# GLA level products for two chunks at once: every second chunk kept backwards and interleaved with its neighbour

## The chip, the core and the metric

The kernel runs on one core of a Trainium2 chip. The metric is the device time of one execution in microseconds (us). The engines are named as in the profile: PE is TensorE (matrix products), PEld its weight load, DVE VectorE, ACT ScalarE, POOL GpSimd, SP the engine that issues all DMAs here.

## What is computed

One inference step of a hybrid decoder layer for 1024 prompt tokens and 8 single sample tokens, all in fp32. Two branches run in parallel, gated linear attention (GLA, 4 heads, key width 128, value width 256) and RWKV-7 (16 heads of 64), and are merged by gates, projected out and normalised.

```python
p = einsum('btd,dn->btn', x, w_in)                      # 1024 -> 9360 columns
p_gla, p_rwkv, p_gate = split(p)
q, k, v, g_a, a_lr = split(p_gla)                       # 512, 512, 1024, 1024, 16
log_a = log_sigmoid(a_lr @ gla_alpha_w2 + gla_alpha_b) / 16
# GLA:    S_t = diag(a_t) S_{t-1} + k_t^T v_t ;  o_t = q_t S_t
# chunked: A[i,j] = sum_d q[i,d] k[j,d] exp(b[i,d] - b[j,d]) for j <= i, b = cumsum(log_a)
#          o = A v + (q exp(b)) S
o_gla = rmsnorm(o_gla) * gla_norm_w * silu(g_a)
# RWKV-7: S_t = S_{t-1}(diag(w_t) - kk_t^T (kk_t a_t)) + v_t^T k_t ;  y_t = S_t r_t
o_rwkv = (groupnorm(y) + bonus) * silu(g_b)
m = sigmoid(gate_a) * (o_gla @ w_up_gla) + sigmoid(gate_b) * (o_rwkv @ w_up_rwkv)
y = layernorm(ALPHA * x + m @ w_out)
```

The final GLA and RWKV states and the last projected RWKV row are outputs too.

## The kernel before

**Halves and stages.** Tokens lie along the free dimension, channels on the partitions. The tokens are done in two halves (`PASS`, line 29): half 0 has 512 prompt tokens and the 8 samples, cut into two tiles of 260 columns; half 1 has 512 prompt tokens in one tile. For each half the plan (`make_plan`, line 1558) lists blocks of 128 output channels of the input projection: RWKV rows, GLA rows (q, k, two of v for each head, later two of the gate g), and the merge gates, which are stored in DRAM (`gate_row`). Each block is 24 fp32r products per token tile (operands are split in a high and a low part: 8 slices of 128 x 3). After both halves of the input projection come the up-projections (GLA half 0, RWKV half 0, GLA half 1, RWKV half 1), then the output projection.

**The order of the work.** It is decided by a planner written in the kernel (`Order`, line 238): each activity is a stream (a Python generator) that yields operations; at each step the planner takes the operation with the best start by its own prices and priorities, and issues it. So any change of an operation moves the order on all engines. All operations are issued from one helper, which is why nearly every line of the profile says L216: groups are told apart by the tiles that they write and read. All DMAs go through SP's queue, in order. Each engine executes its own instructions in order. Buffers are counted: 31 rows of 128 x 520 ("row"), PSUM banks "proj" (2), "big" (3), "pch" (1), "pY" (2).

**One GLA head** (`gla_head`, line 752) runs when its q, k, v rows are projected, one head at a time. It computes the decay a (tile `al`), then the lower triangle AT of the attention matrix of each of four chunks of 128 tokens (`GC`), in levels m = 1, 2, 4, ..., 64 (`LEVELS`). At level m the chunk is cut into blocks of 2m tokens; the queries of a block's second half meet the keys of its first half, each scaled by the decays up to the middle. Afterwards q and k are scaled on to the next level in place. The level's product takes all 128 keys of a chunk as the stationary operand and the 64 queries of the second halves as the moving one:

```python
for x in range(NGC if lv else 0):
    qc = qp_[:, x * P:(x + 1) * P].rearrange("p (b two m) -> p b two m", two=2, m=m)
    yield self.P.matmul(pl[:, x], km_[:, x * P:(x + 1) * P], qc[:, :, 1, :], start=True, stop=True)
```

Half of the stationary operand (the keys of second halves) is of no use in it. The result's useful blocks are written into AT with a mask (`copy_predicated`, mask `lev`) for m = 1 to 8 (`MASKED = 4`), and block by block for 16, 32 and 64: 4 + 2 + 1 copies. The diagonal and level 1 come without a product, from sums of q x k on VectorE. After the levels, for each chunk: transposes of v and k (`vk`), the products AT x v, S x q and k x v, and the state S.

**The up-projection** (`up_row`, line 1420) multiplies each block's result by a gate. `load_gates` (line 1404) fetches the gates from DRAM once the front parts of all eight RWKV pairs (`fronts`) and all gate rows (`gated`) of half 1 are done, and while 8 rows are spare; a block is not issued before its gate's load is (`yield lambda: self.gts`).

Of the kernel before, what the change touches and what calls it, by code (L numbers as in the profile page):

```python
# [12 lines left out]
I32 = mybir.dt.int32  # L13
U8 = mybir.dt.uint8
AF = mybir.ActivationFunctionType
ALU = mybir.AluOpType
AP = bass.AP
# [10 lines left out]

PASS = [(0, HT + NS, NS, [(0, 260), (260, 260)]), (HT + NS, HT, 0, [(0, 512)])]
GH, GDK, GDV = 4, 128, 256  # L30
# [29 lines left out]
RAWS = 4  # L60
SPARE_ROWS = 8


# [23 lines left out]
LEVELS = [1, 2, 4, 8, 16, 32, 64]  # L87
MASKED = 4
GLA_EPS = 1e-5
# [20 lines left out]
def constants():  # L110
    c = np.zeros((P, CST_W), np.float32)

    def put(name, v):
        o, w = CST[name]
        c[:, o:o + w] = v

    i = np.arange(P)
    put("ident", np.eye(P))
    s, t = i[:, None] % C, i[None, :] % C
    put("gmask", np.concatenate([s < t, s <= t], axis=1))  # L120
    lev = np.zeros((P, 64 * MASKED), np.uint8)
    for n, m in enumerate(LEVELS[:MASKED]):
        ri = np.array([x for x in range(P) if (x // m) % 2 == 1])
        j = i[:, None]
        lev[:, 64 * n:64 * n + 64] = ((j // (2 * m)) == (ri[None, :] // (2 * m))) & ((j // m) % 2 == 0)
    return c, lev, ((i[:, None] // C) == (i[None] // C)).astype(np.float32)
# [277 lines left out]
class Kern(Order):  # L404
# [71 lines left out]
    def setup(self):  # L476
# [42 lines left out]

        self.lev = cp.tile([P, 64 * MASKED], U8, name="lev")  # L520

# [221 lines left out]

    def gla_row(self, c, rows, scale):
        x = yield from self.row(c.n, KEEP)
        rows.append(x)

        def ev(tt, t0, w, q):
            yield self.A.activation(x[:, t0:t0 + w], q, AF.Copy, scale=scale)
        return ev  # L750

    def gla_head(self, c, h, rows, g):
# [11 lines left out]
        for t0, w in c.tiles:  # L764
            pz = yield from self.bank("big", [P, w])
            yield self.P.matmul(pz, self.gw2[:, h * GDK:(h + 1) * GDK], self.alr[:, t0:t0 + w], start=True, stop=True)
            yield A.activation(z[:, t0:t0 + w], pz, AF.Identity, bias=self.pvec("gab", h))
            self.free(pz)
# [5 lines left out]

        AT = AT_.rearrange("p (c t) -> p c t", c=NGC)
        yield E.memset(AT, 0.0)
# [4 lines left out]
        yield E.tensor_mul(u, q[:, :HT], k[:, :HT])  # L781
# [3 lines left out]
        yield E.tensor_mul(u[:, 0::2], km_[:, 0::2], qp_[:, 1::2])  # L785
        yield V.transpose(w, u)
# [4 lines left out]
        for i in range(4):  # L791
            yield V.tensor_add(dd[b[i], :, 0:NGC], r2[b[0], :, i::4], r2[b[2], :, i::4])
        dd = dd[:, :, 0:NGC].unsqueeze(3)
        yield V.copy_predicated(AT, self.ident.bitcast(I32).unsqueeze(1).to_broadcast([P, NGC, P]),
                                dd[:, 0].to_broadcast([P, NGC, P]))
        tot = al[:, :HT]
        for lv, m in enumerate(LEVELS):
            nb = P // (2 * m)
            pl = (yield from self.bank("big", [P, NGC, nb, m])) if lv else None
            wide = lv < MASKED  # L800
# [3 lines left out]
            mk = self.lev[:, 64 * lv:64 * lv + 64] if wide else None  # L804
            av = AT.rearrange("p c (b two m) -> p c b two m", two=2, m=m)
            if m == 1:
                out, dat, mk = av[:, :, :, 1, 0], dd[:, 1].to_broadcast([P, NGC, 64]), \
                    mk.unsqueeze(1).to_broadcast([P, NGC, 64])
            elif wide:
                out, dat = av[:, :, :, 1, :], pl  # L810
                mk = mk.rearrange("p (b m) -> p b m", m=m).unsqueeze(1).to_broadcast([P, NGC, nb, m])
            nt = HT // (2 * m)
            tv = tot.rearrange("p (b two) -> p b two", two=2)
            qv = qp_.rearrange("p (b two m) -> p b two m", two=2, m=m)
            kv = km_.rearrange("p (b two m) -> p b two m", two=2, m=m)
            nt_ = al[:, :nt]
            yield E.tensor_mul(kv[:, :, 0, :], kv[:, :, 0, :], tv[:, :, 1:2].to_broadcast([P, nt, m]))
            yield E.tensor_mul(qv[:, :, 1, :], qv[:, :, 1, :], tv[:, :, 0:1].to_broadcast([P, nt, m]))
            yield E.tensor_mul(nt_, tv[:, :, 0], tv[:, :, 1])
            if wide:  # L820
                yield V.copy_predicated(out, mk, dat)
            else:
                for b in range(nb):
                    s = slice(2 * m * b, 2 * m * b + m)
                    yield self.C.copy(av[s, :, b, 1], pl[s, :, b])
            self.free(*([pl] if lv else [r, r2, dd]))
            tot = nt_


        def vk(x):  # L830
            s = slice(x * P, (x + 1) * P)
            pt = yield from self.bank("big", [P, 3 * P])
            yield self.tr(pt[:, 0:P], v[0][:, s])
            yield self.tr(pt[:, P:2 * P], v[1][:, s])
            yield self.tr(pt[:, 2 * P:], km_[:, s])
            VK = vks[x % 2][:, :3 * P]
            yield A.copy(VK, pt)
            self.free(pt)
            return VK
        VK = yield from vk(0)  # L840
        for x in range(NGC):
            s = slice(x * P, (x + 1) * P)
            VKn = (yield from vk(x + 1)) if x < NGC - 1 else None
            pb = yield from self.bank("big", [P, 4, P])
            po, pS = pb[:, 0:2], pb[:, 2:4].rearrange("p a b -> p (a b)")
            for j in range(2):
                yield self.P.matmul(po[:, j], VK[:, j * P:(j + 1) * P], AT[:, x], start=True, stop=(S is None))
                if S is not None:
                    yield self.P.matmul(po[:, j], S[:, j * P:(j + 1) * P], qp_[:, s], start=False, stop=True)
# [708 lines left out]
    def make_plan(self):  # L1558
        w_in = self.a["w_in"]
        for c in self.ctx:  # L1560
# [15 lines left out]
            for p in range(NPAIR):  # L1576
# [9 lines left out]
                if p % 2 == 0:  # L1586
# [3 lines left out]
                    for n, (off, scale) in enumerate(offs):  # L1590
                        self.add(c, lambda c=c, rows=rows, scale=scale: self.gla_row(c, rows, scale), w_in, off,
                                 (lambda c=c, h=h, rows=rows, g=c.gg[h]:
                                   self.spawn(self.gla_head(c, h, rows, g), "head")) if n == 3 else None)
# [24 lines left out]
    def run_all(self):  # L1618
        self.chained, self.headed, self.decayed = -1, 0, 0
        self.first = ["wa", "x0", "w0", "x1", "x2", "x3", "w1", "x4", "x5", "x6", "x7", "pv", "shift", "w2", "w3", "cst"]  # L1620
        self.has = set()
        self.sampled = self.w_done = False
        self.plan, self.xq, self.ws, self.wo, self.gts, self.l2s = [], [], [], [], [], []
        self.setup()
# [70 lines left out]
```

## Time and profile before

| | us |
|---|---|
| median of 3 runs | 1623.23 |
| lowest, highest | 1619.05, 1623.53 |
| span of the profiled execution | 1622.0 |

No other time is given for the profiled execution than its span; the median lies 1.2 us above it. The mean granted TensorE clock is 0.995.

How to read the profile: a group's row has line, engine, operation, written<-read tiles and shapes, the count, then busy time and mean ns of one, then the idle time before it and what ended it. A row of waits has the engine and tile, what it waited for, then total us, times and the longest. A timeline row has start, duration, engine, operation and, in brackets, the idle time before it. A row of windows has busy time and instruction count of each engine in a stretch. Recorded durations of products overlap, since they are pipelined; what a product costs is read from the distance between starts. One fp32 product appears as two passes, one fp32r product as one.

### The profile page before, as it was taken

Reading aid. Unit: us, or ns where it says so; the run is one execution under the profiler, and the core shown is the slowest. Engines: PE = TensorE matmul, PEld = TensorE weight load, DVE = VectorE, ACT = ScalarE, POOL = GpSimd, SP = SyncE. Lnnn points to the kernel's source line nnn. Section 1 sums busy time; section 2 is a strip of 40 time slices with the busy share of each in tenths; the row PEclk is TensorE's granted clock in tenths of the full one; section 3 lists DMA queues with packets and bytes.
Section 4 is the critical chain, followed back from the end, with each engine's and each line's share of the span. In section 5 each row is a group of like instructions: output and inputs, shape, how many; then the busy total and the mean of one; then the engine's idle time right before and its main releaser. Section 6 shows DMA issues by size and latency. Waiting matters only on the chain.

```text
span 1622.0 us, 29342 instructions
## 1 busy us (share of the span) xinstructions
PE 1571.4 (97%) x10066; PEld 1393.9 (86%) x10066; DVE 1273.1 (78%) x3349; ACT 821.4 (51%) x1929; POOL 124.3 (8%) x205
## 2 busy tenths in 40 slices
PE   8999999999999999999999999999999989999998
PEld 6999999899999998778888877778788879988786
DVE  6788888788888988878777898788886785765555
ACT  5555655566566656553644464436444545544210
POOL 1001200101000001000000011111000100000000
PEclk9999999999999999999999999999999999999999
DMA  9766765587577657664465436644654577888432
GB/s 303 241 216 216 249 224 183 194 275 244 179 227 254 231 170 255 210 177 113 143 200 165 140 123 193 188 135 133 208 170 118 159 223 235 262 286 270 140 112 84
DMA packets 206641, 318.27 MB, mean 196 GB/s; under 512 B 87204, under 2 KB 102573, under 8 KB 206493
## 3 DMA queue, kind: packets, MB, share of 16 engines
q1 hardware_dynamic: 206492, 316.40, 61.3%
q8 instruction: 80, 1.31, 0.3%
q14 instruction: 69, 0.56, 0.1%
HBM read 196.66 MB, written 118.61 MB: 194 GB/s over the span
## 4 chain that ended last, share of the span: by engine, by line
PE 45%; DVE 9%; DMA 6%; ACT 2%; SPq 2%; issue 2%; POOL 0%; POOLq 0%; DVEq 0%; ACTq 0%
PE proj L216 21%; PE big L216 15%; PE pY L216 6%; PE pch L216 3%; DVE Xt L216 2%; DVE row L216 2%; DMA wide<-LD 2%; DVE X L216 2%; SPq L216 2%; DVE wide L216 1%; ACT row L216 1%; DMA wpart<-w 0%; DMA row<-xT 0%; DMA o_gla<-row 0%; DMA wraw<-w_up_gla 0%
## 5 line engine op out<-in xcount | busy, mean ns | idle before, releaser
L216 PE MATMUL proj<-xh,wpart 128*128 128x260 f32 (+1 forms) x3760 | 919.8, 328 | 2.3 <-DMA wpart<-w 2.1
L216 PEld LDWEIGHTS proj<-xh,wpart 128*128 128x128 f32 x3760 | 626.6, 189 | 52.3 <-issue 5.6
L216 PE MATMUL proj<-xl,wpart 128*128 128x260 f32 (+1 forms) x1880 | 618.1, 329 | 0.4 <-DVE xl L216 0.3
L216 PEld LDWEIGHTS proj<-xl,wpart 128*128 128x128 f32 x1880 | 355.8, 189 | 25.3 <-issue 3.4
L216 ACT CAST wpart<-wraw 128x512 fp32r<-128x512 f32 x210 | 130.0, 622 | 115.1 <-PE proj L216 64.6
L216 DVE TENSOR_TENSOR row<-row 128x512 f32<-128x512 f32 (+9 forms) x314 | 160.6, 517 | 11.3 <-DMA row<-state_rwkv 2.7
L216 DVE TENSOR_TENSOR wpart<-wraw,wpart 128x512 fp32r<-128x512 f32 x200 | 139.9, 701 | 36.1 <-ACT wpart L216 33.8
L216 ACT ACTIVATE row<-row 128x512 f32<-128x512 f32 (+5 forms) x229 | 138.6, 612 | 52.6 <-DVE row L216 39.1
L216 DVE TENSOR_TENSOR Xt<-X,wide 128x60 f32<-128x60 f32 (+24 forms) x496 | 111.1, 224 | 21.2 <-DMA wide<-LD 10.6
L216 ACT ACTIVATE s0p<-wide,pc 64x64 f32<-64x64 f32 x256 | 88.1, 344 | 67.1 <-DVE wide L216 59.1
L216 PE MATMUL big<-row 128*128 128x64 f32 (+4 forms) x712 | 114.4, 278 | 5.5 <-DVE row L216 3.1
L216 DVE TENSOR_TENSOR X<-X,Xt 128x60 f32<-128x60 f32 (+24 forms) x496 | 107.1, 216 | 12.0
L216 ACT ACTIVATE row<-proj,omu 128x260 f32<-128x260 f32 (+1 forms) x99 | 54.1, 546 | 120.5 <-PE proj L216 120.1
L216 POOL TENSOR_TENSOR row<-row 128x512 f32<-128x512 f32 (+7 forms) x55 | 58.9, 1073 | 672.4 <-DVE row L216 287.5
L216 PEld LDWEIGHTS big<-row 128*128 128x128 f32 (+1 forms) x712 | 97.3, 191 | 13.8 <-DVE row L216 4.6
L216 DVE SCALAR_TENSOR_TENSOR wide<-pch,pc,s0p 64x64 f32<-64x64 f32 x224 | 63.1, 282 | 30.1 <-PE pch L216 24.6
L216 DVE SCALAR_TENSOR_TENSOR row<-proj,pv,row 128x259 f32<-128x259 f32 (+1 forms) x99 | 56.4, 570 | 31.5 <-ACT tail L216 18.5
L216 ACT COPY row<-big 128x384 f32<-128x384 f32 (+6 forms) x167 | 46.0, 301 | 60.6 <-PE big L216 58.5
L216 PE MATMUL big<-xh,wpart 128*128 128x260 f32 (+1 forms) x288 | 73.5, 336 | 0.0
L383 ACT ACT_TABLE_LOAD x52 | 66.7, 1283 | 0.9
L216 PE MATMUL big<-az,wide 128*128 128x256 f32 x256 | 65.7, 383 | 0.5 <-ACT wide L216 0.5
L216 DVE COPY rh<-pch 128x128 f32<-128x128 f32 x128 | 37.1, 290 | 30.5 <-PE pch L216 28.5
(240 smaller groups left out, 2490.5 us busy)
## 6 DMA issues: line engine op xcount, KB each, us to landing
w<-wpart SPq DMA_DIRECT2D x146, 512.0 KB
wpart<-w SPq DMA_DIRECT2D x146, 512.0 KB
wraw<-w_in SPq DMA_DIRECT2D x146, 256.0 KB
wide<-LD SPq DMA_DIRECT2D x64, 128.0 KB
wraw<-w_up_gla SPq DMA_DIRECT2D x32, 256.0 KB
wraw<-w_up_rwkv SPq DMA_DIRECT2D x32, 256.0 KB
sg<-row SPq DMA_DIRECT2D x16, 260.0 KB
row<-sg SPq DMA_DIRECT2D x16, 260.0 KB
```

The costliest lines, as they stand in the source:

```text
L216: ways.append((eng, lambda call=call: call(out, *args, **kw), price(eng, name, out, args, ins)))
L383: self.nc.scalar.preload_act_table_set(self.table)
```

## The change

**Pairs of chunks.** Two neighbouring chunks of 128 tokens share one storage of 256 columns: chunk 0 has the even columns, in its own order, chunk 1 the odd columns, backwards. Seen in this order, a block's first half in chunk 0 lies where the second half lies in chunk 1. So each level has, for a pair of chunks, 64 useful keys of each chunk, 128 in all, and 64 useful queries of each, 128 in all. The keys are copied into a packed row (`kp`), and one product of 128x128 replaces two of 128x64; half of its result, where keys of one chunk meet queries of the other, is masked away. The moving operand is read with a step of two elements.

**What follows from it.** q, k and the decay are written into the interleaved order by the evacuations (`places`), v with its second chunks backwards, so that the transposes give reversed rows; each evacuation becomes two instructions, with the samples three. The token tiles of half 0 become 256 and 264. Masks cover levels 1 to 32 (`MASKED = 6`), of 256 columns each; level 64 is written with two copies. AT, q and k are read with a step of two by the products and transposes after the levels, and the output of odd chunks is turned round when it is copied from PSUM.

**Gates.** `load_gates` may fetch the first four gates when the front parts of seven of the eight pairs of half 1 are done, and `up_row` no longer holds a block back: the evacuation waits for the gate. `dynamic_dma_scratch_size=1024` is set when the program is made.

In the built program, counted by form: TensorE 8736 instructions before, 8640 after (192 of 128x64 gone, 96 of 128x128 new; the 260-column products become 256 and 264); ScalarE 1931 and 2034, of these table loads 53 and 67; VectorE 3351 and 3353; GpSimd 210 and 223; DMAs the same in number, the mask's of 1536 bytes a partition in place of 256.

```diff
-PASS = [(0, HT + NS, NS, [(0, 260), (260, 260)]), (HT + NS, HT, 0, [(0, 512)])]
+PASS = [(0, HT + NS, NS, [(0, 256), (256, 264)]), (HT + NS, HT, 0, [(0, 512)])]
+EARLY_GATES = 4
-MASKED = 4
+MASKED = 6
...
+    def paired(self, x):
+        return x[:, :HT].rearrange("p (a q e) -> p a q e", q=GC, e=2)
+    def places(self, x, t0, w, q, paired=True):
+        a, n = t0 // (2 * GC), min(w, HT - t0) // (2 * GC)
+        y = self.paired(x) if paired else x[:, :HT].rearrange("p (a e q) -> p a q e", e=2, q=GC)
+        y, z = y[:, a:a + n], q[:, :n * 2 * GC].rearrange("p (a e q) -> p a e q", e=2, q=GC)
+        parts = [(y[:, :, :, 0], z[:, :, 0]), (y[:, :, ::-1, 1], z[:, :, 1])]
+        return parts + ([(x[:, HT:t0 + w], q[:, HT - t0:w])] if t0 + w > HT else [])
+    def strided(self, x, base, *dims):
+        return AP(x.tensor, x.offset + base, [list(x.ap[0]), *(list(d) for d in dims)])
...
-            yield self.A.activation(x[:, t0:t0 + w], q, AF.Copy, scale=scale)
+            for out, src in [(x[:, t0:t0 + w], q)] if paired is None else self.places(x, t0, w, q, paired):
+                yield self.A.activation(out, src, AF.Copy, scale=scale)
...
-            for x in range(NGC if lv else 0):
-                qc = qp_[:, x * P:(x + 1) * P].rearrange("p (b two m) -> p b two m", two=2, m=m)
-                yield self.P.matmul(pl[:, x], km_[:, x * P:(x + 1) * P], qc[:, :, 1, :], start=True, stop=True)
+            nb = HT // (4 * m)
+            kv, qv = (self.strided(x, o, (4 * m, nb), (e, 2), (2, m)) for x, o, e in
+                      ((km_, 0, 2 * m + 1), (qp_, 2 * m, 1 - 2 * m)))
+            if lv:
+                kp = vks[lv % 2][:, :half * P]
+                yield self.C.copy(kp.rearrange("p (b e m) -> p b e m", e=2, m=m), kv)
+            for x in range(half if lv else 0):
+                yield self.P.matmul(pl[:, x], kp[:, x * P:(x + 1) * P], self.strided(
+                    qp_, 2 * GC * x + 2 * m, (4 * m, nb // half), (1 - 2 * m, 2), (2, m)), start=True, stop=True)
...
+            elif lv < MASKED:
+                mk = self.lev[:, 2 * P * lv:2 * P * lv + 2 * P]
+                yield V.copy_predicated(self.strided(AT_, 2 * m, (4 * m, nb), (1 - 2 * m, 2), (2, m)),
+                                        mk.rearrange("p (b e m) -> p b e m", e=2, m=m),
+                                        pl.rearrange("p a (b e m) -> p (a b) e m", e=2, m=m))
             else:
-                for b in range(nb):
-                    s = slice(2 * m * b, 2 * m * b + m)
-                    yield self.C.copy(av[s, :, b, 1], pl[s, :, b])
+                for e in range(2):
+                    s = slice(m * e, m * e + m)
+                    yield self.C.copy(self.paired(AT_)[s, :, m - m * e:2 * m - m * e, e],
+                                      pl[s].rearrange("p a (e m) -> p a e m", e=2)[:, :, e])
+            for y, o, e in ((kv, 2, -1), (qv, 0, 3)):
+                yield E.tensor_mul(y, y, self.strided(tot, o, (4, nb), (e, 2), (0, m)))
...
-                yield self.P.matmul(po[:, j], VK[:, j * P:(j + 1) * P], AT[:, x], start=True, stop=(S is None))
+                yield self.P.matmul(po[:, j], VK[:, j * P:(j + 1) * P], self.paired(AT_)[:, x // 2, :, x % 2],
+                                    start=True, stop=(S is None))
...
-                yield A.copy(v[j][:, s], po[:, j])
+                yield A.copy(v[j][:, s], po[:, j, ::-1] if x % 2 else po[:, j])
...
-        yield lambda: self.ctx[1].fronts == NPAIR and self.ctx[1].gated == NPAIR + 2 * GH
+        yield lambda: self.ctx[1].fronts >= NPAIR - 1
+                    if x == EARLY_GATES:
+                        yield lambda: self.ctx[1].fronts == NPAIR and self.ctx[1].gated == NPAIR + 2 * GH
...
-        yield lambda: self.gts
-        gt, m = self.gts.pop(0)
+        turn = self.ups
+        self.ups += 1
         def ev(tt, t0, w, q):
+            yield lambda: len(self.gts) > turn
+            gt, m = self.gts[turn]
...
-    nc = bacc.Bacc("TRN2", target_bir_lowering=False, num_devices=1)
+    nc = bacc.Bacc("TRN2", target_bir_lowering=False, num_devices=1, dynamic_dma_scratch_size=1024)
```

More of the change, by code (lines that the diff above doesn't have):

```diff
@@ L120, in constants @@
     put("gmask", np.concatenate([s < t, s <= t], axis=1))
-    lev = np.zeros((P, 64 * MASKED), np.uint8)
+    lev = np.zeros((P, MASKED, 2 * P), np.uint8)
     for n, m in enumerate(LEVELS[:MASKED]):
-        ri = np.array([x for x in range(P) if (x // m) % 2 == 1])
-        j = i[:, None]
-        lev[:, 64 * n:64 * n + 64] = ((j // (2 * m)) == (ri[None, :] // (2 * m))) & ((j // m) % 2 == 0)
+        _, b, e, _ = (x.reshape(-1) for x in np.indices((2, P // (2 * m), 2, m)))
+        lev[:, n] = (i[:, None] // (2 * m) == b) & (i[:, None] // m % 2 == e)
+    lev = lev.reshape(P, -1)
     return c, lev, ((i[:, None] // C) == (i[None] // C)).astype(np.float32)
@@ L518, in setup @@
         self.mg = [[self.dr.tile([P, PASS[i][1]], F32, name=f"mg{i}{k}") for k in range(NK)] for i in range(2)]
-        self.lev = cp.tile([P, 64 * MASKED], U8, name="lev")
+        self.lev = cp.tile([P, 2 * P * MASKED], U8, name="lev")
         self.onesr = cp.tile([P, P], F32R, name="onesr")
@@ L766, in gla_head @@
             yield self.P.matmul(pz, self.gw2[:, h * GDK:(h + 1) * GDK], self.alr[:, t0:t0 + w], start=True, stop=True)
-            yield A.activation(z[:, t0:t0 + w], pz, AF.Identity, bias=self.pvec("gab", h))
+            for out, src in self.places(z, t0, w, pz):
+                yield A.activation(out, src, AF.Identity, bias=self.pvec("gab", h))
             self.free(pz)
@@ L784, in gla_head @@
         yield V.tensor_reduce(r[:, 0], self.blocks32(w), mybir.AxisListType.X, ALU.add)
-        yield E.tensor_mul(u[:, 0::2], km_[:, 0::2], qp_[:, 1::2])
+        half, four, two = NGC // 2, (4, HT // 4), [(2 * GC, NGC // 2), (2, GC // 2)]
+        yield E.tensor_mul(self.strided(u, 0, *two, (GC + 1, 2)),
+                           self.strided(km_, 0, (2 * GC, half), (4, GC // 2), (3, 2)),
+                           self.strided(qp_, 2, (2 * GC, half), (4, GC // 2), (-1, 2)))
         yield V.transpose(w, u)
@@ L792, in gla_head @@
             yield V.tensor_add(dd[b[i], :, 0:NGC], r2[b[0], :, i::4], r2[b[2], :, i::4])
-        dd = dd[:, :, 0:NGC].unsqueeze(3)
-        yield V.copy_predicated(AT, self.ident.bitcast(I32).unsqueeze(1).to_broadcast([P, NGC, P]),
-                                dd[:, 0].to_broadcast([P, NGC, P]))
+        d0, d1 = (dd[:, i, 0:NGC].rearrange("p (a e) -> p a e", e=2).unsqueeze(2) for i in range(2))
+        yield V.copy_predicated(AT_.rearrange("p (a q e) -> p a q e", q=GC, e=2),
+                                self.ident.bitcast(I32).unsqueeze(1).unsqueeze(3).to_broadcast([P, half, GC, 2]),
+                                d0.to_broadcast([P, half, GC, 2]))
@@ new lines, in gla_head @@
+            kv, qv = (self.strided(x, o, (4 * m, nb), (e, 2), (2, m)) for x, o, e in
+                      ((km_, 0, 2 * m + 1), (qp_, 2 * m, 1 - 2 * m)))
+            pl = (yield from self.bank("big", [P, half, P])) if lv else None
+            if lv:
[4 more added lines that the diff above has]
+                    qp_, 2 * GC * x + 2 * m, (4 * m, nb // half), (1 - 2 * m, 2), (2, m)), start=True, stop=True)
@@ L832, in vk @@
             pt = yield from self.bank("big", [P, 3 * P])
-            yield self.tr(pt[:, 0:P], v[0][:, s])
-            yield self.tr(pt[:, P:2 * P], v[1][:, s])
-            yield self.tr(pt[:, 2 * P:], km_[:, s])
+            for j in range(2):
+                yield self.tr(pt[:, j * P:(j + 1) * P], v[j][:, s])
+            yield self.tr(pt[:, 2 * P:], self.paired(km_)[:, x // 2, :, x % 2])
             VK = vks[x % 2][:, :3 * P]
@@ L1420, in up_row @@
     def up_row(self, c, n, x):
-        yield lambda: self.gts
-        gt, m = self.gts.pop(0)
+        yield from ()
+        turn = self.ups
+        self.ups += 1
         def ev(tt, t0, w, q):
+            yield lambda: len(self.gts) > turn
+            gt, m = self.gts[turn]
             s = slice(t0, t0 + w)
@@ L1590, in make_plan @@
                     for n, (off, scale) in enumerate(offs):
-                        self.add(c, lambda c=c, rows=rows, scale=scale: self.gla_row(c, rows, scale), w_in, off,
+                        self.add(c, lambda c=c, rows=rows, scale=scale, n=n: self.gla_row(c, rows, scale, n < 2), w_in, off,
                                  (lambda c=c, h=h, rows=rows, g=c.gg[h]:
```

36 lines of the change are left out of this document (11 added, 25 removed).

## The prediction

> **What bounds the kernel now.** I read the page first (busy shares, slices), then the windows by stage, then what TensorE waits for, then single products in the timeline.
>
> ```profile
> span 1622.0 us, 29342 instructions
> ...
> PE 1571.4 (97%) x10066; PEld 1393.9 (86%) x10066; DVE 1273.1 (78%) x3349; ACT 821.4 (51%) x1929; POOL 124.3 (8%) x205
> ...
> PE   8999999999999999999999999999999989999998
> ...
> PEclk9999999999999999999999999999999999999999
> DMA  9766765587577657664465436644654577888432
> ```
>
> TensorE is the full row: nine tenths or more in all slices but three, at full clock, while VectorE, ScalarE and the DMA engines keep reserves.
>
> ```profile
> core 0: us, PE busy (x) PEld busy (x) DVE busy (x) ACT busy (x) POOL busy (x), PEclk, DMA share, GB/s
> 0.00:640.00 640.00, 625.54 (x4910) 596.50 (x4911) 536.57 (x1467) 384.09 (x968) 62.99 (x107) 1.00 0.70 230
> 640.00:1304.00 664.00, 643.33 (x3433) 533.52 (x3432) 538.49 (x1499) 320.37 (x742) 57.28 (x94) 1.00 0.54 163
> ```
>
> These are the two token halves of the input projection, in which all eight GLA heads lie. In both, TensorE has some 14 to 21 us without work and VectorE has over 100 (640.0 less 536.6; 664.0 less 538.5). So whatever leaves TensorE's stream shortens the span, unless it comes back as a wait. The waits that there are:
>
> ```profile
> PE big L216 <- DVE row L216: 3.1, 5, 1.0
> ...
> PE pY L216 <- ACT xh L216: 2.4, 1, 2.4
> PE big L216 <- ACT row L216: 2.2, 2, 1.9
> PE proj L216 <- DMA wpart<-w: 2.1, 2, 1.4
> PE big L216 <- ACT part L216: 1.7, 2, 0.9
> ...
> PE big L216 <- ACT As L216: 1.1, 1, 1.1
> ```
>
> No single wait is large: TensorE's idle time is 1622.0 - 1571.4 = 50.6 us, in many small pieces. The first and the third row hold what the GLA level products (tile "big" from tile "row") wait for, 5.3 us at most.
>
> **The change: the level products.** Levels m = 2 to 64 use 6 x 4 = 24 products of 128x64 for each head and half, 192 in all; the changed program has 6 x 2 = 12 of 128x128, 96 in all. The trace has two passes for each fp32 product:
>
> ```profile
> L216 PE MATMUL big<-row 128*128 128x64 f32 x384 | 51.1, 272 | 5.0 <-DVE row L216 2.7 <-DVE Xt L216 2.0
> ```
>
> The busy time of this group overlaps its neighbours, so I take the distance between starts. The first fence is a level of 128x64 products, the second the 128x128 products behind the levels:
>
> ```profile
> 902.40 1.00 PE L216 MATMUL big<-row 128*128 128x64 f32 x8
> 903.24 0.27 PE L216 MATMUL big<-cons,Sp 128*64 128x128 f32 x1
> ```
>
> ```profile
> 762.07 0.38 PE L216 MATMUL big<-row 128*128 128x128 f32 x2
> 762.29 0.39 PE L216 MATMUL big<-row,S 128*128 128x128 f32 x2
> 762.52 0.39 PE L216 MATMUL big<-row 128*128 128x128 f32 x2
> ```
>
> Eight passes of 64 columns take 903.24 - 902.40 = 0.84 us, 0.105 each; two passes of 128 take 0.22 to 0.23, 0.11 each. Twice the columns for the same time. So 384 x 0.105 = 40.3 us become 192 x 0.111 = 21.3 us: 19.0 us less. If the 64-column pass also costs 0.111 (the pass after such a group starts late), it is 192 x 0.111 = 21.3. I take 20 us off TensorE, half in each half of the tokens.
>
> **What the trace does not show: a spread operand.** The new products read their moving operand with a step of two elements, and so do the 64 products with AT and the 56 with the state; 32 transposes of k read their stationary operand so. The 0.11 is from packed operands. The nearest spread row is the level above (902.40, m = 2: runs of two elements, then two skipped): 64 columns in 0.105 us, 1.64 ns a column. From below, the new pass costs 0.11, as packed; from above, 128 x 1.64 = 0.21, twice that. There are (96 + 64 + 56) x 2 = 432 such passes, so the term lies between 0 and 432 x 0.10 = 43 us. I take 0, since the level with the runs of two takes no longer a pass than packed ones do. [...]
>
> **The copy ahead of each product.** Each of the 6 x 8 = 48 level steps now copies its part of k (128x256) into a packed row, 35 times on ScalarE and 13 times on VectorE in the changed program, and the products wait for it.
>
> ```profile
> L216 ACT COPY row<-pY 64x256 f32<-64x256 f32 x63 | 23.1, 367 | 42.8 <-PE pY L216 42.3
> L216 DVE TENSOR_TENSOR row<-row 128x256 f32<-128x256 f32 x113 | 48.5, 440 | 3.0 <-PE big L216 2.7
> ```
>
> By these a copy takes 0.37 to 0.44 us. TensorE executes in order, so if a product waits, the projection products behind it wait too. The bounds are nothing (other products are queued ahead, as they are now) and 48 x 0.37 = 17.8 us (each copy fully exposed). Today the steps already wait for one producer, VectorE's scaling of q, and that costs at most 5.3 us in all; a second producer that is ready earlier (the copy reads k, which is scaled before q) I take at half of it, 2.7 us.
>
> **VectorE and ScalarE.**
>
> ```profile
> L216 DVE COPY_PREDICATED row<-lev,big x24: 415/426/741, 92.1 to 1232.8; 128x256 f32<-128x256 uint8 x24
> L216 DVE COPY_PREDICATED row<-lev,pair x8: 723/731/1306, 88.2 to 1225.6; 128x256 f32<-128x256 uint8 x8
> ```
>
> Masked writes of AT grow from three to five levels of this size for each head: 16 more, at 0.43 to 0.74 us; and those that are there may go from 0.43 to 0.74 with their step of two. At most 16 x 0.74 + 24 x 0.31 = 19 us over both halves, and 13 x 0.44 = 6 for copies: 13 us in each half against the 100 us of reserve that VectorE has there. It costs TensorE nothing that the copy term does not hold. If that cover were gone, it would be 25 us. The scalings of q and k keep count and size.
>
> ```profile
> L216 ACT ACTIVATE row<-proj 128x260 f32<-128x260 f32 x48 | 18.4, 383 | 13.3 <-PE proj L216 12.6
> L216 ACT ACTIVATE row<-proj 128x512 f32<-128x512 f32 x24 | 14.3, 596 | 34.5 <-PE proj L216 34.4
> L383 ACT ACT_TABLE_LOAD x52 | 66.7, 1283 | 0.9
> ```
>
> ScalarE's evacuations of q, k, v and the decay become two or three pieces (forward chunk, reversed chunk, samples): the program has 136 of the GLA rows' evacuations in place of 72, and 28 of the decay's in place of 12. By the two rows a piece costs a fixed (383 - 260 x 0.845) = 163 ns, with 0.845 ns an element from (596 - 383)/252, so 80 x 0.163 = 13 us on an engine that idles half the time; TensorE fills a 512-column bank with 24 products, 0.23 us apart in the next fence, in 5.5 us, and has a second bank. I take nothing, and the same for reading or writing a chunk backwards, which no row shows: at twice the time it would still be far below those 5.5 us. The 16 masked levels replace 56 small copies by 16. The order in the changed program has 14 more table loads, 14 x 1.283 = 18 us of ScalarE. Exposed in full they would cost TensorE 18. What TensorE waits for ScalarE today (row 2.2, part 1.7, As 1.1: 5.0 us, with 52 loads) scales to 5.0 x 14/52 = 1.3, which I take.
>
> **The gates and the rest.** Four gate rows are loaded and put through the sigmoid some 500 products before the up-projection begins, from SP's queue, ahead of weight loads. Each is 260 KB, about 1.6 us at that stage's 163 GB/s; the DMA engines are at 0.54 there, and today's whole wait for weights is 2.1 us, so I take nothing; the bound is 4 x 1.6 = 6. The up-projection's products are no longer recorded behind a gate; the evacuation waits instead, and holds its PSUM bank. Does TensorE gain by it? This is its entry into the up-projection:
>
> ```profile
> 1303.93 0.39 PE L216 MATMUL proj<-xh,wpart 128*128 128x512 f32 x1
> 1304.16 0.28 PE L216 MATMUL pY<-xh,wpart 128*128 128x260 f32 x1
> ...
> 1308.32 0.39 PE L216 MATMUL pY<-xh,wpart 128*128 128x260 f32 x1 [2.44 <-ACT xh L216]
> 1310.17 0.59 PE L216 MATMUL pY<-xl,wpart 128*128 128x260 f32 x1 [1.47 <-DVE xl L216]
> 1310.55 0.64 PE L216 MATMUL pY<-xh,wpart 128*128 128x260 f32 x2
> 1310.99 0.42 PE L216 MATMUL pY<-xl,wpart 128*128 128x260 f32 x1
> ```
>
> The first product follows the last projection product at once (0.23 us), and what stops it is xh, the operand loaded anew, not a gate. The change leaves xh where it is: nothing gained. The token tiles 256 + 264 in place of 260 + 260 hold the same 520 columns: nothing. The mask table grows sixfold to 196 KB, under 1 us of DMA at the start, with weights queued behind it: nothing.
>
> **The sum.** 1622.0 - 20 (products) + 2.7 (copies) + 1.3 (table loads) = 1606.0 us of span. The median of the three runs, 1623.2 us (1619.1 to 1623.5), is 1.2 above the profiled span; with it, 1607 us.
>
> **The rivals.**
>
> *The spread operand is read at half rate* (slower). For it: no row shows a step of two at 128 columns. Against: the runs of two at m = 2. Price 43 us: 1607 + 43 = 1650. It decides from 16 us on, where a spread pass takes over 0.11 + 16/432 = 0.15 us. [...] Chance 0.08.
>
> *The copies come late* and TensorE hands back what it saved: each level step exposed, 17.8 in place of 2.7 us, gives 1607 + 15 = 1622, no change; with the bound of the table loads in part too it goes some us beyond. For it: levels form a strict chain (copy, product, scaling, next level), and single waits of up to 1.0 and 1.9 us for these tiles are in the rows above. Against: in the timeline the groups stand between projection products, with 5.3 us of wait in 48 steps, and the order again puts them apart. Chance 0.16.
>
> *The entry into the up-projection tightens as well.* With gates loaded before it, SP's queue and ScalarE are freer for xh there. The two waits are 2.44 + 1.47 us, and behind them three products take 0.65 us in place of 0.36, for eight such triples 2.3 us more: 6.2 in all. 1607 - 6 = 1601. For it: the loads of gates and of xh share the queue in that stage. Against: xh's buffer is free only after the last projection product. Chance 0.10.
>
> That the change does not do what it says is out: the built program has 96 level products for 192.
>
> **How the numbers follow.** The forecast, 1607 us, has 0.66. What this kernel's measurement can tell from no change is about 0.3%, 4.9 us: faster is below 1618.3, slower above 1628.1. The forecast case is faster nearly always (0.61 of 0.66, 0.04 the same, 0.01 slower), the third rival always (0.10); of the late copies 0.03 is faster, 0.07 the same and 0.06 slower; the half rate is slower (0.08). That makes 0.74 faster, 0.11 the same, 0.15 slower. The range: below, the upper saving of 21.3, no added waits and the tighter entry, 1622.0 + 1.2 - 21.3 - 6 = 1596; above, the late copies at 1622 to 1623. It leaves out the half rate and the worst of the late copies.
>
> **What would show it.** In the changed kernel's trace: 192 passes of 128x128 for the level products with starts 0.11 us apart (at 0.2 the first rival is true); TensorE's waits for tile "row" from ScalarE or VectorE at 5 to 10 us (over 20: the second); both projection stages about 8 us shorter each, and the stage from the last GLA head to the end the same length. I am wrong if the stages keep their length with TensorE idle in them, or if TensorE stays as busy as before.

## The result and the profile after

The changed kernel takes 1599.4 us (median of 4 runs, 1596.9 to 1607.8) against 1622.9 for the kernel before (1619.1 to 1623.5): ratio 0.987, 95% interval 0.984 to 0.989. In a second set, beside the last experiments, it was 1600.0 (1595.8 to 1608.7; 1597 to 1603 had been expected) against 1618.9, ratio 0.989 (0.987 to 0.991). 1607 us was forecast, range 1596 to 1623. The profiled span went from 1622.0 to 1596.0 us. First the page of the kernel after. Then the windows of the two halves of the input projection, before and after (columns as in the prediction), each cut at the first product of 512 columns and at the last product of the projection:

```profile
span 1596.0 us, 29099 instructions
...
PE 1550.1 (97%) x9874; PEld 1371.0 (86%) x9874; DVE 1282.5 (80%) x3351; ACT 855.9 (54%) x2032; POOL 123.5 (8%) x218
...
PE   8999999999999999999999999999999999999998
```

```profile
0.00:657.08 657.08, 642.62 (x5047) 612.51 (x5047) 546.74 (x1501) 392.20 (x989) 62.99 (x107) 1.00 0.70 229
657.08:1303.93 646.85, 626.18 (x3296) 517.43 (x3295) 528.25 (x1465) 312.20 (x721) 57.28 (x94) 1.00 0.54 161
```

```profile
0.00:644.45 644.45, 629.99 (x4924) 600.31 (x4925) 550.58 (x1519) 401.51 (x1041) 56.36 (x114) 1.00 0.71 231
644.45:1282.84 638.39, 619.03 (x3224) 508.48 (x3222) 536.50 (x1462) 336.65 (x767) 64.36 (x101) 1.00 0.56 169
```

TensorE is 21.3 us less busy (1571.4 to 1550.1), 12.6 of them in the first half and 7.2 in the second, and as full as before: 45.9 us of idle time against 50.6. The products came out as forecast. From the timeline, level steps of four passes and the row behind each:

```profile
1050.98 0.69 PE L217 MATMUL big<-row 128*128 128x128 f32 x4
1051.41 0.50 PE L217 MATMUL big<-part,headsr 128*128 128x512 f32 x1
...
1056.88 0.72 PE L217 MATMUL big<-row 128*128 128x128 f32 x4
1057.53 0.50 PE L217 MATMUL big<-part,headsr 128*128 128x512 f32 x1
...
1063.32 0.62 PE L217 MATMUL big<-row 128*128 128x128 f32 x4
1063.69 0.49 PE L217 MATMUL proj<-xh,wpart 128*128 128x512 f32 x1
```

These are three level steps; 1051.41 - 1050.98 = 0.43 us and 0.37 us for four passes, 0.09 to 0.11 each by this count (the row behind starts 0.03 us after the fourth pass); the middle step takes 0.65 and does so with packed operands too (below). But the place that decides turned out to be the entry into the up-projection. The windows around it, after:

```profile
1260.00:1280.00 20.00, 19.41 (x102) 16.13 (x101) 13.87 (x45) 13.06 (x28) 0.42 (x4) 1.00 0.82 271
1280.00:1300.00 20.00, 17.85 (x119) 16.75 (x119) 18.13 (x60) 8.83 (x16) 0.00 (x0) 0.91 0.63 201
1300.00:1320.00 20.00, 19.41 (x161) 19.14 (x160) 11.98 (x24) 10.76 (x22) 0.00 (x0) 1.00 0.68 195
```

TensorE is busy through it, and the next section shows that this is not a matter of course.

### The profile page after: what moved, and what is told of

The parts are those of the page before. It is cut to its first block, busy times and chain, and to the rows that moved or that the text cites. A ratio compares the mean times of both kernels' runs of the same rounds, so it can differ in the third digit from the quotient of the medians.

```text
span 1596.0 us, 29099 instructions
## 1 busy us (share of the span) xinstructions
PE 1550.1 (97%) x9874; PEld 1371.0 (86%) x9874; DVE 1282.5 (80%) x3351; ACT 855.9 (54%) x2032; POOL 123.5 (8%) x218
## 4 chain that ended last, share of the span: by engine, by line
PE 60%; DVE 23%; DMA 6%; SPq 4%; issue 4%; ACT 3%; POOL 0%; DVEq 0%; POOLq 0%; ACTq 0%
PE proj L217 30%; PE big L217 19%; DVE row L217 8%; PE pY L217 7%; PE pch L217 4%; SPq L217 4%; DVE Xt L217 3%; DVE X L217 3%; DVE wide L217 2%; DVE wpart L217 2%; DMA wide<-LD 1%; DVE az L217 1%; DMA wraw<-w_in 1%; ACT row L217 1%; DVE pair L217 1%
## 5 line engine op out<-in xcount | busy, mean ns | idle before, releaser
L217 PE MATMUL proj<-xh,wpart 128*128 128x256 f32 (+2 forms) x3744 | 915.5, 328 | 2.4 <-DMA wpart<-w 2.0
L217 PE MATMUL proj<-xl,wpart 128*128 128x264 f32 (+2 forms) x1872 | 611.6, 327 | 0.9 <-DVE xl L217 0.7
L217 DVE TENSOR_TENSOR wpart<-wraw,wpart 128x512 fp32r<-128x512 f32 x207 | 142.3, 689 | 38.1 <-ACT wpart L217 37.3
L217 DVE TENSOR_TENSOR row<-row 128x512 f32<-128x512 f32 (+10 forms) x302 | 164.0, 549 | 7.3 <-ACT row L217 2.4
L217 POOL TENSOR_TENSOR row<-row 128x256 f32<-128x256 f32 (+5 forms) x67 | 67.2, 1005 | 575.8 <-DVE row L217 238.6
L217 ACT ACTIVATE row<-proj,omu 128x256 f32<-128x256 f32 (+1 forms) x99 | 54.1, 547 | 98.6 <-PE proj L217 98.4
L217 PE MATMUL big<-row 128*128 128x128 f32 (+3 forms) x520 | 96.4, 287 | 9.4 <-DVE Xt L217 4.0
L217 DVE SCALAR_TENSOR_TENSOR row<-proj,pv,row 128x255 f32<-128x255 f32 (+1 forms) x99 | 56.2, 568 | 26.6 <-ACT tail L217 17.5
L217 PE MATMUL big<-xh,wpart 128*128 128x512 f32 (+2 forms) x304 | 74.8, 329 | 0.0
L217 ACT COPY row<-big 128x128 f32<-128x128 f32 (+5 forms) x134 | 38.5, 317 | 64.8 <-PE big L217 56.5
L217 PE MATMUL big<-part,headsr 128*128 128x512 f32 x128 | 55.7, 440 | 7.3 <-ACT part L217 3.4
```

Of the source, the lines that this page charges most:

```text
L217: ways.append((eng, lambda call=call: call(out, *args, **kw), price(eng, name, out, args, ins)))
```

## The experiments

Theory at the start: the gain is TensorE's shorter stream and would come from the products alone. Rivals: the gates bring a part of it; the order brings it by luck.

**Half the products, nothing else.**

```diff
-            for x in range(NGC if lv else 0):
-                qc = qp_[:, x * P:(x + 1) * P].rearrange(...)
-                yield self.P.matmul(pl[:, x], km_[:, x * P:(x + 1) * P], qc[:, :, 1, :], ...)
+            for x in range(0, NGC if lv else 0, 2):
+                qc = qp_[:, x * P:(x + 2) * P].rearrange(...)
+                yield self.P.matmul(pl[:, x:x + 2]..., km_[:, x * P:(x + 1) * P], qc[:, :, 1, :], ...)
```

> The kernel before with half the level products and nothing else: one product of 128x128 for two neighbouring chunks, the keys of the first chunk against the queries of both (the second chunk's keys are left out of the result). No interleaving, no copies, no new masks, no gates moved. Theory (the gain is TensorE's stream getting shorter): 96 products of two passes less, 19 to 21 us, so 1602 to 1604 us against 1623, ratio 0.987 to 0.989. Rival (a good part of the gain comes from the gates or from a luckier order): 1610 to 1617 us. Rival (the overheads of pairing cost nothing and the products alone bring all 24 us): 1599.

Measured: 1623.1 us against 1621.1, ratio 1.002 (1.000 to 1.003). Not one of the expected numbers: half of the level products are gone (TensorE is busy 1554.3 us in place of 1571.4), and the time has not moved. TensorE's own timeline at the end of the input projection says where they went (in brackets the idle time and what ended it):

```profile
1284.15 0.27 PE L216 MATMUL big<-cons,tail 128*99 128x128 f32 x1
1295.94 0.79 PE L216 MATMUL big<-part,headsr 128*128 128x512 f32 x1 [11.52 <-DVE part L216]
1298.87 1.52 PE L216 MATMUL big<-part,headsr 128*128 128x512 f32 x2 [2.13 <-DVE part L216]
1300.18 0.42 PE L216 MATMUL big<-cons,tail 128*99 128x128 f32 x1
1305.35 1.91 PE L216 MATMUL big<-Xt,L 128*128 128x32 f32 x8 [4.74 <-DVE Xt L216]
1307.07 0.51 PE L216 MATMUL big<-cons,tail 128*99 128x128 f32 x1
1307.24 0.57 PE L216 MATMUL pY<-xh,wpart 128*128 128x260 f32 x1
```

TensorE is through the input projection at 1284, 20 us earlier than before (1304), then waits 11.5 + 2.1 + 4.7 us for VectorE, and its first up-projection product (pY from xh) starts at 1307, later than before.

**Pairs alone:** the changed kernel with `load_gates` and `up_row` as they were.

```diff
+        yield lambda: self.ctx[1].fronts == NPAIR and self.ctx[1].gated == NPAIR + 2 * GH   # load_gates
-        yield lambda: self.ctx[1].fronts >= NPAIR - 1
-                    if x == EARLY_GATES: ...
+        yield lambda: self.gts                                                              # up_row
+        gt, m = self.gts.pop(0)
```

> The changed kernel with the gates' part undone: pairs of chunks alone. Theory: 1598 to 1606 us, the same as the changed kernel within its scatter. Rival (the gates bring the 6 us that came beyond the products' 20): 1605 to 1609 us.

Measured: 1622.2 us, ratio 1.001 (0.999 to 1.002). The whole of the pairing, without the gates, brings nothing. Its timeline has the same hole, and its windows too:

```profile
1287.55 0.27 PE L217 MATMUL big<-cons,tail 128*99 128x128 f32 x1
1302.84 0.79 PE L217 MATMUL big<-part,headsr 128*128 128x512 f32 x1 [15.03 <-DVE part L217]
1305.89 1.52 PE L217 MATMUL big<-part,headsr 128*128 128x512 f32 x2 [2.25 <-DVE part L217]
1307.21 0.41 PE L217 MATMUL big<-cons,tail 128*99 128x128 f32 x1
1312.37 1.91 PE L217 MATMUL big<-Xt,L 128*128 128x32 f32 x8 [4.75 <-DVE Xt L217]
```

```profile
1280.00:1300.00 20.00, 7.82 (x35) 6.09 (x33) 18.00 (x63) 10.21 (x18) 0.00 (x0) 0.75 0.73 247
1300.00:1320.00 20.00, 10.16 (x51) 8.66 (x52) 10.12 (x29) 8.47 (x15) 0.00 (x0) 0.57 0.35 83
```

In these 40 us TensorE works 18.0 us, in the changed kernel 37.3; the granted clock falls to 0.57, and what follows the waits is slow as well (0.79 us recorded for one product of "part", against 0.39 for the one at 1287.31). VectorE's timeline shows what it does in the meantime: the small steps of the last RWKV pair (X, Xt), one behind the other, and only then the tile "part" for which TensorE waits:

```profile
1301.82 0.17 DVE L217 TENSOR_TENSOR Xt<-X,wide 128x8 f32<-128x8 f32 x1
1302.02 0.17 DVE L217 TENSOR_TENSOR X<-X,Xt 128x8 f32<-128x8 f32 x1
1302.10 0.68 DVE L217 TENSOR_TENSOR part<-row,part 128x512 fp32r<-128x512 f32 x1
```

The up-projection's products could fill the hole, but none stand there in TensorE's order: a block is held back until a gate's load is issued, and gates are loaded only when two counts are full, `fronts` and `gated`. `fronts` is full early: in the kernel `front` raises it ahead of the products `gg` and of the X steps, and VectorE writes the last pair's `gg` from 1265.51 on. What comes last is `gated`, the last gate row times its own sigmoid. Here are that row's sigmoid on ScalarE, its multiplication on VectorE and the first X step of the last pair, before and with pairs alone, from the timelines of the two engines:

```profile
1294.72 0.63 ACT L216 ACTIVATE row<-row 128x512 f32<-128x512 f32 x1
1295.80 0.69 DVE L216 TENSOR_TENSOR row<-row 128x512 f32<-128x512 f32 x1
1297.82 0.19 DVE L216 TENSOR_TENSOR Xt<-X,wide 128x31 f32<-128x31 f32 x1 [1.33 <-DMA wide<-LD]
```

```profile
1279.18 0.19 DVE L217 TENSOR_TENSOR Xt<-X,wide 128x31 f32<-128x31 f32 x1 [0.41 <-issue]
1280.91 0.63 ACT L217 ACTIVATE row<-row 128x512 f32<-128x512 f32 x1
1302.70 0.68 DVE L217 TENSOR_TENSOR row<-row 128x512 f32<-128x512 f32 x1
```

Before, the multiplication came 2 us ahead of the chain of X steps, and the chain (1298 to 1323) ran beside the up-projection. With pairs alone the sigmoid is 14 us earlier than before, but the chain has already begun, and the planner ranks its steps higher (`PRIO`: "pair" 0.4, "gate" 0.05). So the multiplication of 0.7 us stands behind the whole chain of 23 us, and the gates with it. With half the products it is the same: sigmoid at 1273.14, multiplication at 1295.80, chain from 1270.55 to 1295.12. No run moves this multiplication alone; that it is the half of the condition that came last is read from the kernel and these traces. SP's queue shows the first gate load of the kernels before, after, and with pairs alone, in this order:

```profile
1297.07 0.33 SPq L216 DMA_DIRECT2D row<-sg  x1
```

```profile
1163.94 0.43 SPq L217 DMA_DIRECT2D row<-sg  x1
```

```profile
1310.57 0.43 SPq L217 DMA_DIRECT2D row<-sg  x1
```

Before, the first load went out at 1297, 7 us ahead of the first up-projection product at 1304.16. With pairs alone it went out at 1310.57, 23 us behind the last product of the input projection (1287.09). In the changed kernel the multiplication stands behind the chain as well (1301.12), and it does no harm, since four gates are in hand.

**Token tiles alone:** the kernel before with the token tiles of the changed kernel. The work is the same in amount, and the planner's order moves.

```diff
-PASS = [(0, HT + NS, NS, [(0, 260), (260, 260)]), (HT + NS, HT, 0, [(0, 512)])]
+PASS = [(0, HT + NS, NS, [(0, 256), (256, 264)]), (HT + NS, HT, 0, [(0, 512)])]
```

Expected: 1623 us but for what the order brings by luck, put at 4 us either way (1619 to 1627); outside of that, the tile sizes themselves would count. Measured: 1622.0 us against 1621.1, ratio 1.001 (0.999 to 1.002). So neither the tiles nor this other order bring anything. This kernel does not give the right outputs, for a reason that stays open, so only its time is used.

**Gates alone:** the kernel before with the changed `load_gates` and `up_row`.

```diff
-        yield lambda: self.ctx[1].fronts == NPAIR and self.ctx[1].gated == NPAIR + 2 * GH   # load_gates
+        yield lambda: self.ctx[1].fronts >= NPAIR - 1
+                    if x == EARLY_GATES: ...
-        yield lambda: self.gts                                                              # up_row
-        gt, m = self.gts.pop(0)
         def ev(tt, t0, w, q):
+            yield lambda: len(self.gts) > turn
+            gt, m = self.gts[turn]
```

> The kernel before with the gates' part alone: four gates fetched early, the up-projection's blocks no longer held back behind a gate. Theory (TensorE's entry into the up-projection waits for xh, not for a gate): 1620 to 1625 us, no change. Rival (the early gates tighten the entry): 1615 to 1618 us.

Measured: 1612.3 us, ratio 0.995 (0.994 to 0.997), faster than either theory allowed. Its order is that of the kernel before on all engines up to the first early gate, which SP issues at 1172.09. Yet on that common order its profiled run already leads by 8.8 us at the last transfer ahead of that gate (SP's timeline, before and gates alone):

```profile
1179.66 1.14 SPq L216 DMA_DIRECT2D wide<-Sp  x2
```

```profile
1170.90 1.14 SPq L217 DMA_DIRECT2D wide<-Sp  x2
```

So much do two single runs differ on one order. Of the 1622.0 - 1606.1 = 15.9 us between the two spans, 7.1 come after that. From the last product of the input projection to the end it is 1622.0 - 1303.9 = 318.1 us before and 1606.1 - 1293.3 = 312.8 with the gates: 5.3 us behind the entry, near the size of the third rival (6 us). This is one pair of traces; how the median's 8.7 us divide stays open.

**Which half of the gates' part.** Both runs start from the changed kernel; the first has the old `up_row`, the second the old `load_gates`.

```diff
+        yield lambda: self.gts                          # first run: up_row
+        gt, m = self.gts.pop(0)
         def ev(tt, t0, w, q):
-            yield lambda: len(self.gts) > turn
-            gt, m = self.gts[turn]
```

```diff
-        yield lambda: self.ctx[1].fronts >= NPAIR - 1   # second run: load_gates
+        yield lambda: self.ctx[1].fronts == NPAIR and self.ctx[1].gated == NPAIR + 2 * GH
-                    if x == EARLY_GATES: ...
```

> The changed kernel with up_row as it was: a block of the up-projection is again held back until its gate's load is issued, but the first four gates are still fetched early. Theory (without gates the planner has no up-projection products to put ahead of the last pair's norm products, and TensorE waits for VectorE's chain; four gates in hand give four blocks, some 23 us of products, as cover): 1597 to 1603 us, like the changed kernel. Rival (what matters is that blocks are not held back): 1612 to 1622 us.

Measured: 1604.9 us against 1618.0, ratio 0.992 (0.991 to 0.994), just outside the number, well on the theory's side of the rival.

> The changed kernel with load_gates as it was: gates are fetched only when the last pair's front is done, but a block is not held back, its evacuation waits for the gate and holds the PSUM bank. Theory: two or three blocks fit the banks, 12 to 17 us of cover for a chain of some 20 us, so most of the gain stays: 1602 to 1610 us. Rival (early fetching is what matters): 1615 to 1622 us.

Measured: 1612.8 us, ratio 0.995 (0.994 to 0.997), between the theory's and the rival's numbers. In its profiled run, the slowest of the seven (1619.6 us), the one large wait at the entry is no longer for a part, but for the evacuation that waits for its gate and holds a PSUM bank:

```profile
1324.65 0.59 PE L217 MATMUL pY<-xh,wpart 128*128 128x264 f32 x1 [8.00 <-DVE row L217]
```

**How much cover.** Two gates in place of four, with blocks held back as before:

```diff
-EARLY_GATES = 4
+EARLY_GATES = 2
```

> The changed kernel with up_row as it was (a block is held back until its gate's load is issued) and two gates fetched early in place of four. Theory (the cover is the blocks whose gates are in hand: two blocks, 2 x 48 x 0.12 = 12 us, for a chain of some 20 us behind the input projection): 6 to 10 us slower than with four gates, 1610 to 1616 us. Rival (it is enough that the up-projection has begun): 1603 to 1606 us, as with four.

Measured: 1614.8 us against 1618.9, ratio 0.997 (0.996 to 0.998), as the theory had it: none, two and four gates in hand give 1.001, 0.997 and 0.992 (each from another set of runs). Part of the hole is back, here in the waits of TensorE from 1240 to 1345 us:

```profile
PE big L217 <- DVE Xt L217: 4.7, 1, 4.7
PE big L217 <- DVE part L217: 4.1, 2, 2.4
```

And the changed kernel, blocks not held back, with no gate kept waiting for the last pair:

```diff
-EARLY_GATES = 4
+EARLY_GATES = 8
```

> The changed kernel with EARLY_GATES = 8, so that no gate waits for the last pair's front any more, only for spare rows. Theory (four gates cover the chain already; what is left at the entry is xh): 1596 to 1602 us, no change. Rival (more cover, more gain): 1590 to 1595 us. Rival (rows taken early are missed by the last pair): 1605 us and more.

Measured: 1602.9 us, ratio 0.991 (0.989 to 0.992): a microsecond above the theory's numbers and no more than four bring. It stays below the third rival's 1605, so nothing shows that the rows held are missed.

**Half the products and the gates.** The saving of the products with its cover, but without the copies, split evacuations, masks and table loads of the pairing.

Its edit is the diff of the half products and the diff of the gates alone, both on the kernel before.

> The kernel before with half the level products (the second chunk's keys are left out of the result, as in the run with half the products alone) and with the gates' part. It has the saving of pairing without its copies, split evacuations, masks and table loads. Theory (saving and cover together make the gain, the overheads cost some 4 us): 1593 to 1599 us, 0 to 5 below the changed kernel. Rival (the interleaving brings something of its own): 1605 to 1612 us. Rival (saving and gates merely add, 0 and -9): 1612 to 1615 us.

Measured: 1597.2 us against 1618.0, ratio 0.988 (0.986 to 0.990), inside the theory's numbers. So saving and cover together make the gain; the interleaving brings nothing of its own, and its overheads are too small to be told (the changed kernel has 0.987 and 0.989). The token tiles and `dynamic_dma_scratch_size` are those of before in this run, so they have no part in the gain.

**The operand with a step of two, and the copies.** Both start from the changed kernel.

```diff
-                yield self.P.matmul(pl[:, x], kp[:, x * P:(x + 1) * P], self.strided(
-                    qp_, 2 * GC * x + 2 * m, (4 * m, nb // half), (1 - 2 * m, 2), (2, m)), start=True, stop=True)
+                yield self.P.matmul(pl[:, x], kp[:, x * P:(x + 1) * P], qp_[:, x * P:(x + 1) * P], start=True, stop=True)
```

> The changed kernel with the moving operand of the level products read packed (128 neighbouring columns of q, which are the wrong ones: AT comes out wrong), all else as it is. Theory (a step of two costs nothing in a product that takes 0.11 us a pass by its weights and its 128 columns): no change against the changed kernel, passes 0.11 us apart in both. Rival (the spread read is dearer): 3 us and more faster, and the changed kernel's passes further apart than these.

Measured: 1604.9 us, ratio 0.991 (0.989 to 0.992) against 0.989 (0.987 to 0.991) for the changed kernel beside it: not faster. Two steps of its timeline, to be laid beside those after:

```profile
1054.03 0.61 PE L217 MATMUL big<-row 128*128 128x128 f32 x4
1054.39 0.48 PE L217 MATMUL big<-part,headsr 128*128 128x512 f32 x1
...
1059.96 0.71 PE L217 MATMUL big<-row 128*128 128x128 f32 x4
1060.62 0.50 PE L217 MATMUL big<-part,headsr 128*128 128x512 f32 x1
```

0.36 us against 0.43 in the first, 0.66 against 0.65 in the second: in these two the step costs at most 0.07 us for four passes, and the time does not show it. This run packs the level products only. For the products with AT and with the state the traces answer: by the median distance between starts, their passes with a step of two (128 and 112) are 0.114 us apart after, and packed before 0.111 and 0.112.

```diff
                 yield self.C.copy(kp.rearrange("p (b e m) -> p b e m", e=2, m=m), kv)
+                yield self.C.copy(kp.rearrange("p (b e m) -> p b e m", e=2, m=m), kv)
```

> The changed kernel with each of the 48 copies ahead of the level products made twice. Theory (the copies lie beside other products; some 0.06 us of each shows): 0 to 4 us slower than the changed kernel. Rival (the copies are exposed): 48 x 0.4 = 19 us slower, 1618 us.

Measured: 1604.6 us, ratio 0.991 (0.990 to 0.993), 4.5 us above the changed kernel's median in the same set, with intervals that overlap: by the medians 48 copies more cost some 0.1 us each; the ends of the intervals allow from nothing to 0.2, but not 0.4.

## Why the prediction came out as it did

The number was right, 1607 against 1599 to 1600, and so was the sign. The working was right in the size of its largest term and wrong in what that term depends on. That the number came out is in part luck: the 20 us of the products bring nothing alone, and they count only because the change also has the gates' part, for which the sum has nothing.

*Products, 20 us off TensorE's stream:* right in size (21.3 us of busy time; the input projection ends 17 to 21 us earlier with half the products, with pairs alone and after). But the step from there to the end time failed: what leaves TensorE's stream was to shorten the span unless it comes back as a wait, and the waits were looked for at the copies and the table loads. It came back at the entry into the up-projection, 18.4 us with half the products and 22.0 with pairs alone. The ratio was 1.002 and 1.001 there; with the gates as well 0.987.

*Gates, "nothing gained":* this is the step that failed. The text looked at the entry as it was, saw xh as the last wait, and stopped there. It did not ask whether the condition on the gates would still be met ahead of the entry in the new order. The trace of before could have made one ask: the first gate load at 1297 was 7 us ahead of the first up-projection product, and the multiplication that it hangs on 2 us ahead of VectorE's chain. It does not show that these two would change places. That is the second rival's outcome, no change, reached by another mechanism than the one named: the wait stood behind the last pair, and not at the copies. The early gates are what prevents it; on top of that the part behind the entry was 5.3 us shorter in the traces of the gates alone, near what the third rival said.

*The signs:* passes 0.11 us apart (after, 0.133 at m = 4) and both halves shorter came true, also in the run with pairs alone, where the time did not move. The loss lay between the stages, where no sign was set. Waits for tile "row" came to 4.1 us, below the 5 to 10 that were named.

*Spread operand, 0 of 43 us:* right to about 2 us: with a step of two the passes with AT and the state were 0.114 us apart, those of the level products 0.114 to 0.116 and at m = 4 0.133, against 0.111 to 0.112 packed, and the packed read of the experiment was no faster. The 0 was an estimate from the level with runs of two (0.105 us a pass of 64 columns), with no row of a step of two behind it.

*Copies 2.7 us, table loads 1.3 us:* the sum of both is within what the runs can tell. A copy took 0.43 us on ScalarE and 0.29 on VectorE, against the 0.37 to 0.44 us taken; TensorE's waits for tile "row" from VectorE and ScalarE are 2.9 and 1.2 us, not more than the 5.3 of before. The table loads were not tried by themselves.

*VectorE's masked writes:* each went to the upper price, 0.74 us, as one view of the tile "lev" shows, and the cover held: VectorE's busy time rose by 4 us in the first half and 8 in the second, and it still has over 90 us of reserve in each.

```profile
L217 DVE COPY_PREDICATED row<-lev,big x40: 719/736/760, 93.2 to 1221.7; 128x256 f32<-128x256 uint8 x40
```

*The 8 us between forecast and result:* the spans differ by 26.0 us where the sum had 16.0. By the traces, 5.1 of the 10.0 more lie ahead of the last product of the input projection, which starts 21.1 us earlier, and 4.9 behind it, near the gain at the entry that the forecast gave to a rival (6 us). Two runs on one order differed by 8.8 us, so this division is not shown.

## What to carry to other kernels

When work leaves the bound engine ahead of a stage boundary, look up on what the next stage's work hangs, and what stands ahead of that on its own engine in the new order. Here the release of the next stage hung on one multiplication of 0.7 us on VectorE. It had stood 2 us ahead of a chain of 23 to 25 us; in the new order it stood behind it, and all of the 20 us were lost, until the next stage's work was freed from that condition. Parts of a change that look like trimmings may be the cover of its main part; run the parts alone and together, since here 1.001 and 0.995 made 0.987.

## What the runs showed of the hardware

A masked write of 128x256 on VectorE took 0.43 us in the median before, where 16 of 24 were written in runs of four elements and more, and 0.74 us in the median of forty after, with a step of two (0.72 at the least). The other eight before, in runs of two elements, took 0.73 us. The scalings of q and k on VectorE (128x256) have a median of 0.42 us in both traces, with the step or without it. By the median distance between starts, an fp32 pass on TensorE took 0.111 to 0.112 us before, with 64 columns or with 128 packed ones, and 0.114 after for those with AT and the state, 128 columns with a step of two; the passes of a level product took 0.114 to 0.116 there, and 0.133 at m = 4. With pairs alone, the granted clock of TensorE was 0.75 and 0.57 in the two stretches of 20 us that hold its 15 us wait. And one order of instructions gave, in two runs, 8.8 us of difference over the first 1180.
